# Padded operands, equal unit offsets and another block order in a hybrid decoder trunk on one core

## The chip, the core and the metric

The kernel runs on one core of one Trainium2 chip. The metric is the device time of one execution in microseconds (us), lower is better. Before the change it is 2168.96 us, the median of 3 runs (2168.53 to 2169.34). The engines are named as in the profile: PE (TensorE), PEld (its weight loads), DVE (VectorE), ACT (ScalarE), POOL (GpSimd), SP (SyncE, which issues the weight DMAs).

## The reference

Four layers act on 256 prompt rows and 8 sample rows of width 1024. Each layer has a feed-forward part, a mixer and a second feed-forward part, each followed by a layer norm. The mixers are: latent attention (layers 0 and 3), a chunked token-mixing MLP (layer 1), and multi-scale pooling (layer 2).

```python
x <- LN(alpha*x + 0.5*SwiGLU_1(x));  x <- LN(alpha*x + Mixer(x));  x <- LN(alpha*x + 0.5*SwiGLU_2(x))

# latent attention, prompt, per query block (8 heads; nope part of width 128, rotary part of width 64)
s = jnp.einsum('bqhc,bkc->bhqk', qlb, c_kv) + jnp.einsum('bqhr,bkr->bhqk', qrb, k_rope)
s = jnp.where(kpos[None, :] <= qpos[:, None], s.astype(jnp.float32) * ATTN_SCALE, NEG_INF)
# latent attention, samples: 1024 cached keys each (256 latent and 64 rotary values), gathered by pages
s_past = jnp.einsum('bqhc,bkc->bhqk', q_lat, past_ckv) + jnp.einsum('bqhr,bkr->bhqk', q_rope, past_kr)

# chunked MLP: u, v of width 3072; v normalised; 8 heads of 384
mixed = jnp.einsum('hij,bnjhd->bnihd', w_s * tril, vc) + b_s.T[None, None, :, :, None]
out = (u * mixed.reshape(B, Sp, D_CMLP)) @ w_out
```

## The kernel before

Activations lie transposed: features on the 128 partitions, and along the free axis 256 prompt columns and 8 sample columns (T = 264, SEQ = 256, DB = 8). Weights stream from memory through four stage tiles (DMA issued by SP, L171). Each is split into units: ACT casts the high part (L201), DVE subtracts to get the low part (L204). The function `mm3` multiplies each weight tile in three matmuls (L276 to L278): high weights by high activations, high by low, low by high. There are 15,144 such matmuls. A unit holds a high and a low half of 128 x 1024 and feeds 24 matmuls in the feed-forward parts. Units go round through six tiles (`NB = 6`); `room` takes tile `slot % NB` and starts `PADS[n]` floats into it (L127).

The program is written out by hand: each engine works through its instructions in the order in which they are issued, and waits by semaphores. Tile pools decide which buffer an operand gets, and so whom a write waits for. Generators interleave the prompt heads and the sample attention: each `yield` hands PE's place to another piece of work. These parts are touched:

- `start` (L391 to L420) loads the input rows and turns them by PE transposes: first the prompt's rows 0 to 127 for all 8 feature blocks k, then for each k the rows 128 to 255 (L407) and the 8 sample rows (L409). `xn` holds the prompt rows, `xs` the sample rows, `bank` and `bank_b` are PSUM tiles. ACT and DVE then make the high and low part per k (L413, L414).
- `cmlp` (layer 1): `gate(t)` (L924 to L940) multiplies for each of 24 blocks t the two prompt chunks of normalised v by the head's matrix (L928), and the 8 sample rows `vs` by the diagonal `diag` (L929).
- `mla` (layers 0 and 3): `rope` writes the rotated key `kr` (L1476) with the 64 rotary features twice, on partitions 0 to 63 and 64 to 127. `scores(h)` (L1533) adds for two query blocks the product of the nope part (L1542), the causal mask (L1543) and the rotary part (L1544), the last on 64 partitions: the lower half for even heads, the upper for odd ones.
- The sample attention handles two groups g of four samples. `flip(g, q)` transposes 32 feature rows of the cached keys of two samples on DVE (L1694 for g = 0, L1697 for g = 1) into a tile `tt`; `nat` and `natr` hold the gathered latent and rotary keys. `score(g)` (L1718) takes 20 such blocks q and issues two matmuls for each (L1740), one per sample, each on 32 weight columns, into its own 32 partitions of `sc`. `where(q)` says which samples and which feature block a q has: q 0 to 9 are all feature blocks of samples 0 and 1, q 10 to 19 those of samples 2 and 3. Up to six flips run ahead of the matmuls. L1787, the product of the probabilities with the keys, uses four column groups in turn.

Of the kernel before, what the change touches and what calls it, by code (L numbers as in the profile page):

```python
# [7 lines left out]
F32 = mybir.dt.float32  # L8
# [111 lines left out]
class Weights:  # L120
# [3 lines left out]
    NB = 6  # L124


    PADS = (0, 12, 16, 28, 36, 52)  # L127

    def __init__(self, nc, stage_pool, unit_pools):
        self.nc = nc  # L130
# [119 lines left out]
def trunk_kernel(ctx: ExitStack, tc: tile.TileContext, i: dict, o: dict, layers=None):  # L250
# [143 lines left out]
    def start():  # L394
        nc.sync.dma_start(out=ident, in_=cst("ident"))
        with tc.tile_pool(name="ld", bufs=1) as ld:
            xn = ld.tile([128, 2, D], F32, name="xn")
            xs = ld.tile([DB, D], F32, name="xs")
            for b in range(2):
                nc.sync.dma_start(out=xn[:, b, :], in_=i["x_prompt"][0, b * 128:(b + 1) * 128, :])  # L400
            nc.scalar.dma_start(out=xs, in_=i["x_sample"].rearrange("b s d -> (b s) d"))
            W.fetch()
            warm(AF.Silu)
            ps = [bank() if k < 6 else bank_b() for k in range(KD)]
            for b in range(2):
                for k, p in enumerate(ps):
                    nc.tensor.transpose(p[:, b * 128:(b + 1) * 128], xn[:, b, k * 128:(k + 1) * 128], ident)  # L407
                    if b == 1:
                        nc.tensor.transpose(p[:, SEQ:T], xs[:, k * 128:(k + 1) * 128], ident[0:DB, 0:DB])  # L409
            for k, p in enumerate(ps):  # L410
                if k == 2:
                    W.pump(1)
                S.copy(out=xh[:, k, 0:T], in_=p[:, 0:T])  # L413
                V.tensor_tensor(out=xl[:, k, 0:T], in0=p[:, 0:T], in1=xh[:, k, 0:T].bitcast(F32), op=ALU.subtract)  # L414

                nc.gpsimd.tensor_tensor(out=x[:, k, :], in0=xh[:, k, 0:T].bitcast(F32), in1=xl[:, k, 0:T].bitcast(F32), op=ALU.add)
            W.pump()
# [344 lines left out]
    def cmlp(l, j, pool, gp, prev):  # L762
        G0, B0, VB0 = 96, 0, 48
        vn = pool.tile([128, 2, DC], F32, name="vn")
        vs = pool.tile([DB, DC], F32, name="vs")
        wst = pool.tile([128, HEADS, 128], F32, name="wst")
        rb = pool.tile([128, HEADS, 136], F32, name="rb")
        bsb = pool.tile([128, HEADS, 136], F32, name="bsb")
        diag = pool.tile([DB, HEADS, DB], F32, name="diag")
        w00 = pool.tile([128, HEADS], F32, name="w00")  # L770
        stat = pool.tile([128, 3, 6, 6], F32, name="stat")
        mv = pool.tile([128, 3, 2], F32, name="mv")
# [1 line left out]
        rows = (128, 128, DB)  # L774

        def v_view(q, c):
            return vs[:, c] if q == 2 else vn[:, q, c]

        with tc.tile_pool(name="vt", bufs=3) as vt, tc.tile_pool(name="vt1", bufs=1) as vt1:
            wn = vt1.tile([128, HEADS, 128], F32, name="wn")  # L780
# [4 lines left out]
            nc.gpsimd.dma_start(out=bsb[:, :, 0:128], in_=i["b_b_s"][j:j + 1].to_broadcast([128, HEADS, 128]))  # L785
            V.memset(mv, 1.0)

            def setup(step):

                if step == 0:  # L790
                    nc.gpsimd.tensor_tensor(out=wn, in0=wn, in1=tril.unsqueeze(1).to_broadcast([128, HEADS, 128]), op=ALU.mult)
                    return
                if step == 3:
                    V.tensor_copy(out=rb[:, :, 128:136], in_=w00.unsqueeze(2).to_broadcast([128, HEADS, DB]))
                    V.tensor_copy(out=bsb[:, :, 128:136], in_=bsb[:, :, 0:1].to_broadcast([128, HEADS, DB]))
                    V.tensor_tensor(out=diag, in0=w00[0:DB].unsqueeze(2).to_broadcast([DB, HEADS, DB]),
                                    in1=ident[0:DB, 0:DB].unsqueeze(1).to_broadcast([DB, HEADS, DB]), op=ALU.mult)
                for hq in range(2):
                    f = slice(hq * 4, hq * 4 + 4)
                    p = bank()  # L800
                    if step == 1:
                        for h in range(4):
                            nc.tensor.transpose(p[:, h * 128:(h + 1) * 128], wn[:, hq * 4 + h, :], ident)
                        S.copy(out=wst[:, f, :].rearrange("p h i -> p (h i)"), in_=p)
                    if step == 2:
                        MM(p, ones, wst[:, f, :].rearrange("p h i -> p (h i)"), start=True, stop=True)
                        S.mul(out=rb[:, f, 0:128], in_=p.rearrange("p (h i) -> p h i", h=4), mul=float(D))
# [31 lines left out]
            for t in range(4, NC_T + 3):  # L839
                if t < NC_T:  # L840
                    new = [(t, bank())]
                    prev.columns(new[0][1], W.take(1)[0])
                else:
                    new = []
                    u_cols(t - NC_T)
                out = turned
                turned = [v_turn(*a) for a in acts]
                acts = v_fix(made[0:2])
                made = made[2:] + new
                for q, p in out:  # L850
                    S.copy(out=vn[:, :, q * 128:(q + 1) * 128], in_=p[:, 0:256].rearrange("p (b d) -> p b d", b=2))
                    V.tensor_copy(out=vs[:, q * 128:(q + 1) * 128], in_=p[0:DB, 256:384])
                if t == NC_T + 2:
                    break
                W.pump(min(t, W.NB))
                W.done(1)
                k, part = divmod(t - 5, 2)
                if part == 1 and 0 <= k < KD:
                    prev.affine(k)
                if part == 0 and 0 < k <= KD:  # L860
                    S.copy(out=xh[:, k - 1, 0:T], in_=x[:, k - 1, :])
                for _, g, vb in acts:
                    S.activation(out=g, in_=g, func=AF.Gelu_apprx_tanh, bias=vb)
                acts = [a[0:2] for a in acts]
                if part == 0 and 0 <= k < KD:
                    prev.normal(k)
                if part == 0 and 0 < k <= KD:
                    nc.gpsimd.tensor_tensor(out=xl[:, k - 1, 0:T], in0=x[:, k - 1, :], in1=xh[:, k - 1, 0:T].bitcast(F32),
                                            op=ALU.subtract)
                for q, _ in out:  # L870
                    if q % 4 == 3:
                        sums.extend((q // 4, r) for r in range(3))
                for a in sums[0:1]:
                    v_stats(*a)
                del sums[0:1]
                if t in (16, 17, 18, 19):
                    setup(t - 16)
# [19 lines left out]
        with tc.tile_pool(name="mx2", bufs=2) as mx2:  # L897
# [4 lines left out]
            def v_rows(q, step):  # L902
# [5 lines left out]
                        nc.sync.dma_start(out=t, in_=i[nm][j:j + 1, c].to_broadcast([DB, 512]))  # L908
                    return
                g, b = gb.pop(q)  # L910
                nc.gpsimd.tensor_tensor(out=g, in0=g, in1=vs[:, c], op=ALU.mult)
                nc.gpsimd.tensor_tensor(out=g, in0=g, in1=b, op=ALU.add)
                nc.sync.dma_start(out=o["cv"][j].rearrange("b s d -> (b s) d")[:, c], in_=g)

# [319 lines left out]
    def mla(l, j, pool, prev, stack):  # L1234
# [9 lines left out]
                mc[nm] = t[:, a - a0:a - a0 + w]  # L1244

        ckv = pool.tile([128, 2, T], F32, name="ckv")
        kr = pool.tile([128, T], F32, name="kr")
        qn = pool.tile([128, HEADS, SEQ], F32, name="qn")
        qr = pool.tile([128, 4, T], F32, name="qr")
        qs = pool.tile([128, HEADS + 3, DB], F32, name="qs")  # L1250
# [33 lines left out]
        with tc.tile_pool(name="pa", bufs=1) as pa, tc.tile_pool(name="pf0", bufs=1) as pf0, \  # L1284
# [2 lines left out]
            load_keys(0)  # L1287
            consts(("rep", "causal", "sel", "own", "new", "blk", "last"), pool)
            nc.gpsimd.memset(mx[:, 0:32], 0.0)
            nc.gpsimd.memset(qs[:, HEADS:, :], 0.0)  # L1290
            nc.gpsimd.memset(olt[:, :, HEADS:, :], 0.0)
            wukt = []
# [169 lines left out]
            def rope(key, src, r, tag, dep):  # L1462
# [8 lines left out]
                @step("o" + key, "m" + key)  # L1471
                def _():
                    t = lnp.tile([128, T], F32, tag=tag, name="rp")
                    V.tensor_tensor(out=t, in0=src(), in1=mc["ct"], op=ALU.mult)
                    V.tensor_tensor(out=sw[key], in0=sw[key], in1=mc["st"], op=ALU.mult)
                    V.tensor_tensor(out=r, in0=t, in1=sw[key], op=ALU.add)  # L1476

            for c in range(4):
                rope(str(c), lambda c=c: qp[c, 2][:, 0:T], qr[:, c, :], ("acc", "accq")[c % 2], f"p{c}2")
            rope("k", lambda: tiles[5], kr, "acc", "v5")  # L1480


            for pair in range(4):
# [33 lines left out]
        with tc.tile_pool(name="pb", bufs=1) as pb, tc.tile_pool(name="pb2", bufs=2) as pb2:  # L1517
# [15 lines left out]
            def scores(h):  # L1533
                kn = st.pop(("k", h))
                p = bank()
                off = 64 * (h % 2)
                rr = slice(off, off + 64)
                for b in range(2):
                    n = 128 * (b + 1)
                    out = p[:, 128 * b:128 * b + n]  # L1540
                    qq = slice(b * 128, (b + 1) * 128)
                    MM(out, qn[:, h, qq], kn[:, 0:n], start=True, stop=False)  # L1542
                    MM(p[:, 256 * b:256 * b + 128], identr, causal, start=False, stop=False)  # L1543
                    MM(out, qr[rr, h // 2, qq], kr[rr, 0:n], start=False, stop=True)  # L1544
                P = pb2.tile([128, 384], F32, tag="P", name="P")
                top = pb2.tile([128, 2], F32, tag="top", name="top")
                sm = pb2.tile([128, 2], F32, tag="sm", name="sm")
# [130 lines left out]
            AHEAD, ROOM = 3, 7  # L1678

            def where(q):  # L1680
                return q // 10 * 2, (q + 8) % 10

            def flip(g, q):

# [31 lines left out]
            def score(g):  # L1716
# [17 lines left out]
                for q in range(20):  # L1734
# [3 lines left out]
                        next(gens["f"])  # L1738
                    for b in range(2):
                        MM(sc[(b0 + b) * 32:(b0 + b + 1) * 32, 0:257], qbd[:, cb, b0 + b, :], tt[:, b, 0:257],  # L1740
                           start=q % 10 == 0, stop=q % 10 == 9)
                    if q % 2:
                        yield
                V.tensor_tensor(out=sc[:, 256:257], in0=sc[:, 256:257], in1=mc["new"], op=ALU.add)
# [210 lines left out]
```

## Time and profile before

| | |
|---|---|
| timed runs, median of 3 | 2168.96 us |
| profiled execution | 2157.06 us |
| its span, first to last instruction | 2155.3 us |
| mean granted clock of PE | 0.989 |
| PE busy, share of the span | 2100.6 us, 97% |
| PEld busy | 2030.7 us, 94% |
| DVE busy | 1591.1 us, 74% |
| ACT busy | 1099.2 us, 51% |
| POOL busy | 278.7 us, 13% |

Matmuls are pipelined: the duration of one record (0.28 us for a weight matmul) is longer than the interval at which the next starts (0.12 us). So intervals are read from starts, or from the pieces of the chain of waits, which lie end to end. A matmul on plain f32 operands appears as two records per instruction; a transpose or a weight matmul appears as one. In the chain, a name with a line and a count is a run of records of that line. In a timeline, the bracket at a row's end gives the engine's idle time before it and what ended that.

### The profile page before, as it was taken

The numbers are of one execution on the slowest core, as the hardware profiler recorded it, in microseconds if no ns is written. First come the engines' busy times: TensorE is split into PE (matmuls) and PEld (weight loads), VectorE is DVE, ScalarE is ACT, GpSimd is POOL, SyncE is SP. The second block draws the span as 40 slices with busy tenths as digits, with TensorE's granted clock in tenths as the row PEclk, the third lists the DMA queues.
The fourth block names the chain that finished last, engine by engine and source line by source line (L and its number), as shares of the span: only waits on it lengthen the run. The fifth ranks groups of instructions, "written<-read, shape, count | busy, mean of one in ns | idle before, by whom it ended". The sixth has DMA issues, their size and how long they took to land.

```text
span 2155.3 us, 41932 instructions
## 1 busy us (share of the span) xinstructions
PE 2100.6 (97%) x17021; PEld 2030.7 (94%) x17021; DVE 1591.1 (74%) x3135; ACT 1099.2 (51%) x1792; POOL 278.7 (13%) x321
## 2 busy tenths in 40 slices
PE   9999899999999999999999999899999999899997
PEld 8999669999999999999999999899999998579997
DVE  5546757886887797668777876998868877758774
ACT  5445636445545565455455444464555455546453
POOL 3002500000000054720000000520000005300001
PEclk9999999999999999999999999999999999999998
DMA  8556505555556544445555645356556556235551
GB/s 258 180 185 215 189 24 186 181 182 181 168 166 206 186 157 143 163 152 160 173 201 161 194 164 201 116 185 194 171 173 189 181 170 243 99 120 181 166 193 44
DMA packets 288850, 366.34 MB, mean 170 GB/s; under 512 B 7729, under 2 KB 226570, under 8 KB 286601
## 3 DMA queue, kind: packets, MB, share of 16 engines
q1 hardware_dynamic: 283200, 337.65, 48.4%
q0 software_dynamic: 5424, 25.95, 3.3%
q8 instruction: 134, 2.20, 0.4%
q14 instruction: 60, 0.48, 0.1%
q10 hardware_dynamic: 32, 0.07, 0.0%
HBM read 361.69 MB, written 2.41 MB: 169 GB/s over the span
## 4 chain that ended last, share of the span: by engine, by line
PE 93%; DVE 3%; ACT 2%; issue 1%; DMA 0%; POOL 0%; DVEq 0%; SPq 0%; ACTq 0%; POOLq 0%
PE bank L276 28%; PE bank L278 28%; PE bank L277 28%; PE bank_b L1740 2%; PE bank L1544 1%; DVE w L204 1%; PE bank L1542 1%; PE bank_b L1787 1%; PE bank L1565 1%; ACT sw L1469 1%; DVE win L1113 1%; PE bank_b L928 1%; PE bank L1528 0%; PE bank L1584 0%; ACT w L201 0%
## 5 line engine op out<-in xcount | busy, mean ns | idle before, releaser
L204 DVE TENSOR_TENSOR w<-stage,w 128x1024 fp32r<-128x1024 f32 x630 | 769.2, 1228 | 228.1 <-ACT w L201 227.0
L201 ACT CAST w<-stage 128x1024 fp32r<-128x1024 f32 x642 | 653.7, 1029 | 271.0 <-PE bank L278 216.4
L276 PE MATMUL bank<-xh,w 128*128 128x266 f32 (+1 forms) x2496 | 718.8, 288 | 2.5 <-ACT w L201 2.5
L278 PE MATMUL bank<-xh,w 128*128 128x266 f32 (+1 forms) x2496 | 716.6, 287 | 1.5 <-DVE w L204 1.5
L277 PE MATMUL bank<-xl,w 128*128 128x266 f32 (+1 forms) x2496 | 715.2, 287 | 0.0
L276 PEld LDWEIGHTS bank<-xh,w 128*128 128x128 f32 x2496 | 475.8, 191 | 3.7 <-ACT w L201 3.0
L278 PEld LDWEIGHTS bank<-xh,w 128*128 128x128 f32 x2496 | 475.0, 190 | 1.9 <-DVE w L204 1.9
L277 PEld LDWEIGHTS bank<-xl,w 128*128 128x128 f32 x2496 | 474.3, 190 | 0.3
L276 PE MATMUL bank<-hh,w 128*128 128x264 f32 x1344 | 381.4, 284 | 0.0
L278 PE MATMUL bank<-hh,w 128*128 128x264 f32 x1344 | 381.1, 284 | 0.0
L277 PE MATMUL bank<-hl,w 128*128 128x264 f32 x1344 | 381.1, 284 | 0.0
L722 ACT ACTIVATE t<-t,gb 128x264 f32<-128x264 f32 x147 | 76.1, 518 | 356.8 <-DVE t L569 356.0
L276 PEld LDWEIGHTS bank<-hh,w 128*128 128x128 f32 x1344 | 253.0, 188 | 0.0
L278 PEld LDWEIGHTS bank<-hh,w 128*128 128x128 f32 x1344 | 253.0, 188 | 0.0
L277 PEld LDWEIGHTS bank<-hl,w 128*128 128x128 f32 x1344 | 252.9, 188 | 0.0
L277 PE MATMUL bank<-zl,w 128*128 128x266 f32 (+1 forms) x736 | 212.0, 288 | 2.4 <-DVE zl L1152 2.4
L276 PE MATMUL bank<-zh,w 128*128 128x266 f32 (+1 forms) x736 | 211.8, 288 | 2.3 <-ACT zh L1148 2.3
L278 PE MATMUL bank<-zh,w 128*128 128x266 f32 (+1 forms) x736 | 211.9, 288 | 1.5 <-DVE w L204 1.5
L564 DVE COPY gb<-bank 128x2 f32<-128x2 f32 x318 | 47.0, 153 | 143.6 <-PE bank L278 143.5
L276 PEld LDWEIGHTS bank<-zh,w 128*128 128x128 f32 x736 | 140.8, 191 | 2.7 <-ACT zh L1148 2.6
L277 PEld LDWEIGHTS bank<-zl,w 128*128 128x128 f32 x736 | 140.4, 191 | 2.7 <-DVE zl L1152 2.6
L278 PEld LDWEIGHTS bank<-zh,w 128*128 128x128 f32 x736 | 140.5, 191 | 1.7 <-DVE w L204 1.7
(388 smaller groups left out, 2781.1 us busy)
## 6 DMA issues: line engine op xcount, KB each, us to landing
stage<-in_ffn_w_down_dram SPq DMA_DIRECT2D x80, 1024.0 KB
stage<-in_ffn_w_gate_dram SPq DMA_DIRECT2D x79, 1024.0 KB
stage<-in_ffn_w_up_dram SPq DMA_DIRECT2D x79, 1024.0 KB
stage<-in_b_w_in_dram SPq DMA_DIRECT2D x24, 1024.0 KB
stage<-in_b_w_out_dram SPq DMA_DIRECT2D x12, 1024.0 KB
stage<-in_a_w_o_dram SPq DMA_DIRECT2D x8, 1024.0 KB
stage<-in_ffn_w_gate_dram SPq DMA_DIRECT2D x10, 512.0 KB
stage<-in_ffn_w_up_dram SPq DMA_DIRECT2D x10, 512.0 KB
```

The costliest lines, as they stand in the source:

```text
L201: nc.scalar.copy(out=h, in_=src)
L204: engine.tensor_tensor(out=l, in0=src, in1=h.bitcast(F32), op=ALU.subtract)
L276: MM(out, wh, xh, start=start, stop=False)
L277: MM(out, wh, xl, start=False, stop=False)
L278: MM(out, wl, xh, start=False, stop=stop)
L564: V.tensor_copy(out=gb, in_=p[:, T:T + 2])
L722: S.activation(out=sg, in_=sg, func=AF.Silu, bias=vg)
L928: MM(pm[:, b * 128:(b + 1) * 128], vn[:, b, d], wst[:, h, :], start=True, stop=True)
L1113: e.tensor_tensor(out=win[q][:, :, H0:E], in0=cur[:, :, H0:E], in1=cur[:, :, H0 - d:E - d], op=ALU.add)
L1469: S.copy(out=w[b * 32:(b + 1) * 32, :], in_=src()[f * 32:(f + 1) * 32, :])
L1542: MM(out, qn[:, h, qq], kn[:, 0:n], start=True, stop=False)
L1740: MM(sc[(b0 + b) * 32:(b0 + b + 1) * 32, 0:257], qbd[:, cb, b0 + b, :], tt[:, b, 0:257], start=q % 10 == 0, stop=q % 10 == 9)
```

## The change

The change has five parts. `PADS` becomes zero for all six unit tiles. In `start` the transposes are grouped: all k of rows 0 to 127, then all k of the sample rows, then all k of rows 128 to 255. In `cmlp`, `vs` and `diag` have 128 partitions, are set to zero by POOL first, and keep their data on partitions 0 to 7; the matmul of L929 then runs over 128 partitions. In `mla` the rotary key is written once to `kr` on partitions 0 to 63 (the rest zero) and once to `kr1` on partitions 64 to 127 (the rest zero), and the rotary matmul runs over all 128 partitions with the key tile of the head's parity. Last, `where` gives q 0 and 1 the same feature block of samples 0, 1 and of samples 2, 3, then q 2 and 3 the next block, and so on; the accumulation flags follow.

```diff
-    PADS = (0, 12, 16, 28, 36, 52)
+    PADS = (0, 0, 0, 0, 0, 0)
...
-            for b in range(2):
-                for k, p in enumerate(ps):
-                    nc.tensor.transpose(p[:, b * 128:(b + 1) * 128], xn[:, b, k * 128:(k + 1) * 128], ident)
-                    if b == 1:
-                        nc.tensor.transpose(p[:, SEQ:T], xs[:, k * 128:(k + 1) * 128], ident[0:DB, 0:DB])
+            for k, p in enumerate(ps):
+                nc.tensor.transpose(p[:, 0:128], xn[:, 0, k * 128:(k + 1) * 128], ident)
+            for k, p in enumerate(ps):
+                nc.tensor.transpose(p[:, SEQ:T], xs[:, k * 128:(k + 1) * 128], ident[0:DB, 0:DB])
+            for k, p in enumerate(ps):
+                nc.tensor.transpose(p[:, 128:256], xn[:, 1, k * 128:(k + 1) * 128], ident)
...
-        vs = pool.tile([DB, DC], F32, name="vs")
+        vs = pool.tile([128, DC], F32, name="vs")
-        diag = pool.tile([DB, HEADS, DB], F32, name="diag")
+        diag = pool.tile([128, HEADS, DB], F32, name="diag")
...
+            nc.gpsimd.memset(vs, 0.0)
+            nc.gpsimd.memset(diag, 0.0)
...
         kr = pool.tile([128, T], F32, name="kr")
+        kr1 = pool.tile([128, SEQ], F32, name="kr1")
...
+            nc.gpsimd.memset(kr[64:128, :], 0.0)
+            nc.gpsimd.memset(kr1[0:64, :], 0.0)
...
-                    V.tensor_tensor(out=r, in0=t, in1=sw[key], op=ALU.add)
+                    if key == "k":
+                        V.tensor_tensor(out=kr[0:64, :], in0=t[0:64, :], in1=sw[key][0:64, :], op=ALU.add)
+                        V.tensor_tensor(out=kr1[64:128, :], in0=t[64:128, 0:SEQ], in1=sw[key][64:128, 0:SEQ], op=ALU.add)
+                    else:
+                        V.tensor_tensor(out=r, in0=t, in1=sw[key], op=ALU.add)
...
-                off = 64 * (h % 2)
-                rr = slice(off, off + 64)
+                rk = (kr, kr1)[h % 2]
...
-                    MM(out, qr[rr, h // 2, qq], kr[rr, 0:n], start=False, stop=True)
+                    MM(out, qr[:, h // 2, qq], rk[:, 0:n], start=False, stop=True)
...
-                return q // 10 * 2, (q + 8) % 10
+                return q % 2 * 2, (q // 2 + 8) % 10
...
-                           start=q % 10 == 0, stop=q % 10 == 9)
+                           start=q < 2, stop=q > 17)
```

At the start of the program PE's order before is this (`xn` the prompt rows, `xs` the sample rows; rows that repeat the pair are left out):

```order
L407 MATMUL bank<-ident,xn 128x128 x6
L407 MATMUL bank_b<-ident,xn 128x128 x2
L407 MATMUL bank<-ident,xn 128x128
L409 MATMUL bank<-ident,xs 128x8
...
L407 MATMUL bank_b<-ident,xn 128x128
L409 MATMUL bank_b<-ident,xs 128x8
L276 MATMUL bank<-xh,w 128x264
```

And now, with the lines of the changed file:

```order
L406 MATMUL bank<-ident,xn 128x128 x6
L406 MATMUL bank_b<-ident,xn 128x128 x2
L408 MATMUL bank<-ident,xs 128x8 x6
L408 MATMUL bank_b<-ident,xs 128x8 x2
L410 MATMUL bank<-ident,xn 128x128 x6
L410 MATMUL bank_b<-ident,xn 128x128 x2
L276 MATMUL bank<-xh,w 128x264
```

The sample transposes have moved ahead of the second half of the prompt's, in one group.

In layer 0's mixer, DVE's order from the rotated key to the first copies into `qbd` before is this (`w` and `tt` are the tiles that flips write, `top` and `sm` belong to the prompt's softmax):

```order
L1476 TENSOR_TENSOR kr<-rp,sw 128x264
L1694 STREAM_TRANSPOSE w<-natr 128x2x256 x2
L1548 TENSOR_REDUCE top<-bank 128x1
L1549 TENSOR_REDUCE top<-bank 128x1
L1550 TENSOR_TENSOR top<-top,rq 128x2
L1647 COPY qlat<-bank_b 128x2x64
L1609 RECIPROCAL sm<-sm 128x2
L1694 STREAM_TRANSPOSE w<-nat 128x2x256
L1694 STREAM_TRANSPOSE tt<-nat 128x2x256 x3
L1724 COPY qbd<-qrep 32x40x8 x2
```

And now (`kr_2253` is the tile `kr1`):

```order
L1485 TENSOR_TENSOR kr<-rp,sw 64x264
L1486 TENSOR_TENSOR kr_2253<-rp,sw 64x256
L1705 STREAM_TRANSPOSE w<-natr 128x2x256 x2
L1559 TENSOR_REDUCE top<-bank 128x1
L1560 TENSOR_REDUCE top<-bank 128x1
L1561 TENSOR_TENSOR top<-top,rq 128x2
L1658 COPY qlat<-bank_b 128x2x64
L1620 RECIPROCAL sm<-sm 128x2
L1705 STREAM_TRANSPOSE w<-natr 128x2x256
L1705 STREAM_TRANSPOSE tt<-natr 128x2x256
L1705 STREAM_TRANSPOSE tt<-nat 128x2x256 x2
L1735 COPY qbd<-qrep 32x40x8 x2
```

One DVE instruction is added, the number of flips and their places among the other instructions stay, and the four rotary blocks (`natr`) are now flipped first for all four samples.

## Rows read from the trace of the kernel before

**Rows 1.** The page: busy totals, and the chain that ended last by engine.

```profile
PE 2100.6 (97%) x17021; PEld 2030.7 (94%) x17021; DVE 1591.1 (74%) x3135; ACT 1099.2 (51%) x1792; POOL 278.7 (13%) x321
...
PE 93%; DVE 3%; ACT 2%; issue 1%; DMA 0%; POOL 0%; DVEq 0%; SPq 0%; ACTq 0%; POOLq 0%
```

**Rows 2.** Timeline of PE at one gate: start us, us, instruction, idle before.

```profile
827.45 0.61 PE L928 MATMUL bank_b<-wst,vn 128*128 128x128 f32 x4
827.99 0.38 PE L929 MATMUL bank_b<-diag,vs 8*128 8x8 f32 x2
828.30 0.39 PE L276 MATMUL bank<-xh,w 128*128 128x264 f32 x1
828.53 0.28 PE L277 MATMUL bank<-xl,w 128*128 128x264 f32 x1
```

**Rows 3.** Timeline of PE: two short passes of full rows, then another.

```profile
231.88 0.37 PE L1397 MATMUL bank_b<-rsq,ones 128*128 128x8 f32 x2
232.10 0.69 PE L1421 MATMUL bank_b<-rsq,ones 128*128 128x264 f32 x2
```

**Rows 4.** Chain of waits in layer 0's mixer: start us, us, what.

```profile
269.58 3.61 PE bank_b L1740 x32
...
308.94 1.73 PE bank L1565 x8
...
316.72 3.59 PE bank_b L1787 x64
```

**Rows 5.** Timeline of PE over one head's prompt scores.

```profile
300.12 0.49 PE L1542 MATMUL bank<-kn,qn 128*128 128x128 f32 x2
300.36 0.30 PE L1543 MATMUL bank<-causal,identr 128*128 128x128 f32 x1
300.60 0.48 PE L1544 MATMUL bank<-kr,qr 64*128 64x128 f32 x2
301.01 0.70 PE L1542 MATMUL bank<-kn,qn 128*128 128x256 f32 x2
...
302.33 1.13 PE L1528 MATMUL bank<-ckv,stage 128*128 128x256 f32 x4
```

**Rows 6.** Timeline of ACT: the copy into qbd.

```profile
256.81 1.55 ACT L1722 COPY qbd<-qrep 32x320 f32<-32x320 f32 x2
```

**Rows 7.** Windows of PE: us, busy (instructions), clock, DMA share, GB/s; three units, then six.

```profile
568.52:571.47 2.95, 2.95 (x26) 1.00 1.03 338
571.47:574.46 2.99, 2.99 (x26) 1.00 0.88 297
580.40:583.33 2.93, 2.93 (x26) 1.00 1.07 346
568.52:586.30 17.78, 17.78 (x147) 1.00 0.71 224
```

**Rows 8.** Timeline of DVE: flips of the first and of the second half.

```profile
270.35 1.30 DVE L1694 STREAM_TRANSPOSE tt<-nat 128x512 f32<-128x512 f32 x2
...
280.55 2.03 DVE L1697 STREAM_TRANSPOSE tt<-w 128x256 f32<-128x256 f32 x6
```

**Rows 9.** Timeline at the start.

```profile
10.52 1.23 DVE L204 TENSOR_TENSOR w<-stage,w 128x1024 fp32r<-128x1024 f32 x1 [1.40 <-ACT w L201]
...
11.81 0.59 PE L276 MATMUL bank<-xh,w 128*128 128x264 f32 x1
...
12.42 0.42 PE L278 MATMUL bank<-xh,w 128*128 128x264 f32 x1
```

**Rows 10.** POOL by shapes, 243 to 336 us: zeros of qbd.

```profile
L1515 POOL MEMSET qbd<- 128x1280 f32 x1 | 1.2, 1163 | 0.0
```

**Rows 11.** Windows: us, busy of PE, PEld, DVE, ACT, POOL, clock, DMA share, GB/s.

```profile
273.50:276.95 3.45, 1.26 (x8) 0.92 (x9) 2.00 (x10) 0.99 (x4) 0.00 (x0) 1.00 0.01 2
276.95:280.40 3.45, 2.83 (x13) 1.54 (x13) 3.40 (x12) 1.88 (x3) 0.19 (x1) 0.51 0.01 3
727.00:760.00 33.00, 33.00 (x268) 32.73 (x268) 31.18 (x71) 22.19 (x41) 8.30 (x9) 1.00 0.59 176
```

More of the change, by code (lines that the diff above doesn't have):

```diff
@@ L776, in v_view @@
         def v_view(q, c):
-            return vs[:, c] if q == 2 else vn[:, q, c]
+            return vs[0:DB, c] if q == 2 else vn[:, q, c]
         with tc.tile_pool(name="vt", bufs=3) as vt, tc.tile_pool(name="vt1", bufs=1) as vt1:
@@ L795, in setup @@
                     V.tensor_copy(out=bsb[:, :, 128:136], in_=bsb[:, :, 0:1].to_broadcast([128, HEADS, DB]))
-                    V.tensor_tensor(out=diag, in0=w00[0:DB].unsqueeze(2).to_broadcast([DB, HEADS, DB]),
+                    V.tensor_tensor(out=diag[0:DB], in0=w00[0:DB].unsqueeze(2).to_broadcast([DB, HEADS, DB]),
                                     in1=ident[0:DB, 0:DB].unsqueeze(1).to_broadcast([DB, HEADS, DB]), op=ALU.mult)
@@ L851, in cmlp @@
                     S.copy(out=vn[:, :, q * 128:(q + 1) * 128], in_=p[:, 0:256].rearrange("p (b d) -> p b d", b=2))
-                    V.tensor_copy(out=vs[:, q * 128:(q + 1) * 128], in_=p[0:DB, 256:384])
+                    V.tensor_copy(out=vs[0:DB, q * 128:(q + 1) * 128], in_=p[0:DB, 256:384])
                 if t == NC_T + 2:
@@ L910, in v_rows @@
                 g, b = gb.pop(q)
-                nc.gpsimd.tensor_tensor(out=g, in0=g, in1=vs[:, c], op=ALU.mult)
+                nc.gpsimd.tensor_tensor(out=g, in0=g, in1=vs[0:DB, c], op=ALU.mult)
                 nc.gpsimd.tensor_tensor(out=g, in0=g, in1=b, op=ALU.add)
@@ L1475, in _ @@
                     V.tensor_tensor(out=sw[key], in0=sw[key], in1=mc["st"], op=ALU.mult)
-                    V.tensor_tensor(out=r, in0=t, in1=sw[key], op=ALU.add)
+                    if key == "k":
[3 more added lines that the diff above has]
+                        V.tensor_tensor(out=r, in0=t, in1=sw[key], op=ALU.add)
             for c in range(4):
                 rope(str(c), lambda c=c: qp[c, 2][:, 0:T], qr[:, c, :], ("acc", "accq")[c % 2], f"p{c}2")
-            rope("k", lambda: tiles[5], kr, "acc", "v5")
+            rope("k", lambda: tiles[5], None, "acc", "v5")
             for pair in range(4):
```

## Prediction

> **What bounds the kernel now.** I read the totals first, then the chain of waits by engine, then the timeline at each edited line, then windows over whole weight units. The totals show TensorE (PE) busy for 97% of the span, and the chain that ended last is PE for 93% [rows 1]. So time is saved only where PE itself issues sooner, and VectorE (DVE) matters where it is late for PE. DMA carries 0% of the chain. The sum below is made against the profiled execution, 2157.06 us (span 2155.3), and carried over as a difference to the median of the runs, 2168.96.
>
> **1. Gate rows padded (L929).** The 8-row matmul stands between 128-row ones. From the first pass of L928 to the second matmul after L929 lie 828.53 − 827.45 = 1.08 us [rows 2], for four passes of L928, two of L929 (each fp32 instruction here is two records) and one weight matmul. What would it be without gaps? A pass of 128 rows and 8 columns takes half of 232.10 − 231.88 = 0.22, that is 0.11 us [rows 3]; a pass of 256 columns 1.73 / 8 = 0.216, so one of 128 columns 0.108 [rows 4]; the weight matmul 17.78 / 144 = 0.12 [rows 7]. That is 4 × 0.108 + 2 × 0.11 + 0.12 = 0.77, and 1.08 − 0.77 = 0.31 goes, with loads hidden. L929 has 48 records, 24 instructions, all in layer 1: 24 × 0.30 = **7.2 us**. Ends: 0 (loads stay exposed) to 8. What is late next there is PE's own next matmul.
>
> **2. Rope keys padded (L1544).** One head's prompt scores take 302.33 − 300.12 = 2.21 us [rows 5]. Contiguous, five passes of 128 columns (two L1542, one L1543, two L1544) and four of 256 plus one L1543 are 5 × 0.108 + 4 × 0.216 + 0.108 = 1.51. So 0.70 us a head, a little more if L1543, one record, is shorter than I count. There are 8 heads in each of two layers, 16 × 0.70 = 11.2. Head 1 gains nothing: the sample scores behind it start when ScalarE has filled qbd at 258.36 [rows 6], and PE starts them at 258.45 already. That takes 2 × 0.70 off; a few heads end on sample matmuls of 32 columns, where a change of shape stays, about −0.3. With the upside of L1543, **10.0 us**; ends 0 and 12.8 (0.80 × 16).
>
> A rule of the Trainium skill speaks against both terms: "TensorE: Matmul & The Clock Gate", section "Part 3: Packing small matmuls", says that a weight load overlaps running matmuls only when its row group differs; a 128-row load would then never hide, and both terms would be zero. The trace disagrees: in the L1565 run each full 128-row pass takes 0.216 us with its load inside, while the 64-row pass starts 300.60 − 300.36 = 0.24 us after L1543, a single pass of 128 columns [rows 4, 5].
>
> **3. Sample scores (L1740).** The edit of `where` lets two successive key blocks q use all four column groups in turn instead of two. Now 16 instructions take 3.61 us, 0.226 each; L1787, which goes through four groups in turn, takes 3.59 for 32, 0.112 each [rows 4]. There are 320 records, 160 instructions: 160 × 0.114 = 18.2 us at most. Not all is reached, for the operands are made by DVE. A flip costs 1.30 / 2 = 0.65 us a block in the first half and 2.03 / 3 = 0.68 in the second [rows 8], three times what PE will need for one (0.226). Walking through one layer with these durations and DVE's order: in the first half PE waits for q9 and q11 (0.4) and for q18 and q19, whose flips stand behind the row maxima of head 2 (1.1); in the second half q0 to q3 are already paced by flips (0.7 of the 0.9 lost), and q11 to q13 now are (0.9). That leaves 9.1 − 3.1 = 6.0 a layer, **12.0 us**; ends 0 (flips pace everything) and 18.2. The order of samples changes which keys are wanted when, but before the second half's flips the DMA share is 0.01 already [rows 11].
>
> **4. Pads to 0.** The six unit tiles now start at equal offsets. The trace shows that the interval of matmuls depends on the slot and repeats from round to round: six units of 24 matmuls take 17.78 us, the quickest slot 2.93 and the slowest 2.99 [rows 7], or 122.1 to 124.6 ns a matmul. The slots differ only in address. With one offset, all six become alike; the distance from the moving tile xh to the weights becomes that of the first slot, 2.95. Then 17.78 − 6 × 2.95 = 0.08, which is 0.5 ns a matmul; with the finer times of these starts 0.7 ns, over the 5,520 matmuls on xh and xl: 2.9 to 3.9 us. I take **3.5**. The matmuls on hh and zh, zl I leave at nothing. Ends: every unit on xh like the quickest, −1.35 ns, 7.5 us gained; like the slowest, +1.2 ns, 6.5 us lost.
>
> The page "SBUF — State Buffer", section "SBUF: two separate sides", says that of the engines only VectorE and GpSimd hold each other up and PE waits on no one. By that rule the pads are worth nothing and the sum is 3.5 us smaller; the unit windows show 0.06 us between slots that it leaves unexplained.
>
> **5. First transposes.** Now the last pair ends as the first weight matmul starts, 11.81. The low weights are finished by DVE at 10.52 + 1.23 = 11.75; the matmul on these, the third, starts at 12.42 [rows 9]. With the 8-row loads grouped I expect the transposes to end before that, and DVE's 11.75 is late next: the third matmul gains up to 0.67, and later casts keep some of it. I take **0.3**, ends 0 and 0.67.
>
> **Costs.** The keys' sum becomes two DVE instructions of half the rows, ahead of the first flips, with the queries' matmuls between those and the first sample score: nothing; without that cover not more than a flip's 0.65 us a layer. The zeros of kr and kr1 stand on GpSimd before work nobody waits for. The zeros of vs: 1.16 us for 1280 elements [rows 10] makes 2.8 for 3072, in front of the layer's mean subtraction; PE is busy 33.00 of 33.00 us there [rows 11]. In all I take **−0.3**, ends 0 and −2.
>
> Sum: 7.2 + 10.0 + 12.0 + 3.5 + 0.3 − 0.3 = 32.7 us. Profiled execution 2157.1 − 32.7 = 2124.4; median 2169.0 − 32.7 = 2136.3.
>
> The clock adds a blur. After one PE-poor stretch (1.26 busy of 3.45 us) the granted clock was 0.51, its lower level of 1.2 GHz, for 3.45 us with PE 2.83 busy [rows 11]. At the upper level half of that would do. So a stretch costs up to 1.4 us; shorter waits may remove one, more idle between blocks may add one: ±3.
>
> **Rivals.**
> (a) Padded rows buy nothing, because loads stay exposed. Terms 1 and 2 go: 2136.3 + 17.2 = 2153.5. For it: the rule above. Against: full-row passes back to back, long and short ones [rows 3, 4]. Chance 0.06.
> (b) The flips pace PE through all sample scores: term 3 falls to about 3, 2145. For it: 0.65 against 0.226. Against: DVE has idle time between blocks, and other PE work stands between them. Chance 0.09.
> (c) Addresses decide nothing (the rule of term 4 as a mechanism): 2140. Against: the repeating slot times. Chance 0.13.
> (d) Slower. Equal offsets bring the moving tile and the weights of every family to a bad distance. The price is 15,144 weight matmuls × 1 ns = 15.1 us per ns. From 2139.8 without term 4, it passes 2173.3 (slower by 0.2%) at 2.2 ns more on all of them; at 2.5 ns it is 2178. For it: an address effect of 2.5 ns is seen between slots. Against: the slowest slot seen lies 1.2 ns over the mean, and no family would have to leave what was seen. Chance 0.04.
> My forecast, with clock and small terms: 0.68, own range 2127 to 2145.
>
> **Numbers.** Predicted 2136. To the own range (a) and (b) add the upper end: 2124 to 2151. A change under 0.2% (4.3 us) can't be told from none here; slower: (d), 0.04; within 0.2%: all three large terms failing at once, 0.04; faster 0.92.
>
> **What would show it.** In the new profile: no gap around the gate's third matmul (0.77 for the stretch that took 1.08); the head's scores about 1.5 us; a run of 16 sample instructions near 1.8 us where flips are ready; unit windows on xh all near 2.95; the third weight matmul before 12. The forecast is wrong if 128-row loads stay visible around L929 and L1544, if DVE ends nearly every wait in the sample scores, or if unit windows come out above 3.0.

## The result, and the profile after

The changed kernel took 2132.81 us (median of 4 runs, 2131.80 to 2133.66) beside 2169.15 us for the kernel before (2168.53 to 2171.03): ratio 0.9831, 95% interval 0.9814 to 0.9848, or 36.3 us less. Forecast were 2136 and 32.7 us less. Timed once more, the changed kernel stayed at 2132.19, but the kernel before came to 2155 to 2163 in four later sets, and the same comparison gave 0.9861 (0.9841 to 0.9882), 30 us by the ratio. The two first profiles differ by only 2157.06 − 2133.66 = 23.4 us; for the profiled execution the forecast was 2124.4. Much of what follows is about why the kernel before differs from one set of runs to the next.

The totals of the page, and the chain by engine, which answer to [rows 1]:

```profile
PE 2072.2 (97%) x17021; PEld 2014.4 (94%) x17021; DVE 1593.9 (75%) x3137; ACT 1098.6 (52%) x1792; POOL 281.2 (13%) x327
...
PE 92%; DVE 4%; ACT 2%; issue 1%; DMA 0%; SPq 0%; POOL 0%; DVEq 0%; ACTq 0%; POOLq 0%
```

PE is busy 28.4 us less than before and still 97% of the span; DVE's share of the chain went from 3% to 4%.

The gate in PE's timeline [rows 2]:

```profile
820.01 0.61 PE L932 MATMUL bank_b<-wst,vn 128*128 128x128 f32 x4
820.46 0.29 PE L933 MATMUL bank_b<-diag,vs 128*128 128x8 f32 x2
820.60 0.37 PE L276 MATMUL bank<-xh,w 128*128 128x264 f32 x1
820.80 0.28 PE L277 MATMUL bank<-xl,w 128*128 128x264 f32 x1
```

From the first pass of L932 to the second matmul behind the gate it is 820.80 − 820.01 = 0.79 us, where it was 1.08. The forecast had 0.77. The weight loads (PEld) of the short matmul and of the one behind it, before and then now:

```profile
827.99 0.29 PEld L929 LDWEIGHTS bank_b<-diag,vs 8*128 8x128 f32 x2
828.30 0.19 PEld L276 LDWEIGHTS bank<-xh,w 128*128 128x128 f32 x1
...
820.35 0.30 PEld L933 LDWEIGHTS bank_b<-diag,vs 128*128 128x128 f32 x2
820.57 0.19 PEld L276 LDWEIGHTS bank<-xh,w 128*128 128x128 f32 x1
```

Before, each of these loads begins together with its matmul (827.99 and 828.30). Now it begins ahead of it, by 0.11 and 0.03 us, while the passes in front still run.

One head's prompt scores in PE's timeline [rows 5]:

```profile
297.43 0.49 PE L1553 MATMUL bank<-kn,qn 128*128 128x128 f32 x2
297.68 0.31 PE L1554 MATMUL bank<-causal,identr 128*128 128x128 f32 x1
297.82 0.44 PE L1555 MATMUL bank<-kr,qr 128*128 128x128 f32 x2
298.09 0.60 PE L1553 MATMUL bank<-kn,qn 128*128 128x256 f32 x2
298.34 0.41 PE L1554 MATMUL bank<-causal,identr 128*128 128x128 f32 x1
298.59 0.65 PE L1555 MATMUL bank<-kr,qr 128*128 128x256 f32 x2
299.07 0.38 PE L1540 MATMUL bank<-ckv,stage 128*128 128x256 f32 x1
```

It takes 299.07 − 297.43 = 1.64 us; before 2.21, forecast 1.51. The rotary pass now starts 0.14 us after the mask's, not 0.24.

Runs of sample scores in the chain of waits of layer 0 (start us, us, what), to compare with the first piece of [rows 4]:

```profile
260.33 2.41 PE bank_b L1751 x24
...
277.55 2.82 PE bank_b L1751 x13
...
289.92 1.51 PE bank_b L1751 x23
...
296.06 1.44 PE bank_b L1751 x24
```

The last run has 12 instructions in 1.44 us, 0.120 each, about half of the 0.226 before; the third has 0.131. The first two are slower. The first ran at the lower clock (2.41 us for 12), which will come up. The second lies in another stretch at that clock (0.50 from 275.9 to 282.7 us), in which DVE with its flips was busy 3.35 of the first 3.40 us; so the clock slows it, and probably the flips too.

Unit windows of PE on xh, the same units as in [rows 7], then six together:

```profile
561.66:564.60 2.94, 2.94 (x27) 1.00 1.03 342
564.60:567.54 2.94, 2.94 (x27) 1.00 0.90 301
573.42:576.36 2.94, 2.94 (x27) 1.00 1.05 349
561.66:579.30 17.64, 17.64 (x147) 1.00 0.71 228
```

All are 2.94 now, and six take 17.64 instead of 17.78.

The start, as in [rows 9]:

```profile
10.44 1.22 DVE L204 TENSOR_TENSOR w<-stage,w 128x1024 fp32r<-128x1024 f32 x1 [1.14 <-ACT w L201]
...
10.46 0.59 PE L276 MATMUL bank<-xh,w 128*128 128x264 f32 x1 [0.89 <-ACT w L201]
...
11.72 0.59 PE L278 MATMUL bank<-xh,w 128*128 128x264 f32 x1 [0.45 <-DVE w L204]
```

The first weight matmul starts 1.35 us earlier, the third 0.70.

One place stands out as a wait. The first row maximum of head 0 (L1559) on DVE, in the timeline of all engines:

```profile
248.59 0.65 PE L1555 MATMUL bank<-kr,qr 128*128 128x256 f32 x2
...
249.64 0.95 POOL L1281 DMA_INDIRECT w<-in_cache_kv_latent_dram,idx  x1 [0.30 <-issue]
250.59 0.77 POOL L535 TENSOR_TENSOR x<-mean,x 128x264 f32<-128x264 f32 x1
251.44 0.74 POOL L536 TENSOR_TENSOR x<-x,negr 128x264 f32<-128x264 f32 x1
252.02 0.29 DVE L1559 TENSOR_REDUCE top<-bank 128x1 f32<-128x128 f32 x1 [3.76 <-PE bank L1540]
...
253.14 1.08 PE L1669 MATMUL bank_b<-qlat,c_rep 128*128 128x72 f32 x8 [2.60 <-issue]
```

PE ends the head's scores at 249.24 and DVE has nothing else to do, yet its instruction starts at 252.02, near the end of GpSimd's second tensor instruction (252.18 as recorded; times on GpSimd are rough). In the first profile of the kernel before, the same wait was 1.14 us. PE, which needs a copy that DVE makes right after (L1658), idles 2.60 us before L1669. And this is what the clock did next (windows: us, busy of PE, PEld, DVE, ACT, POOL, granted clock, DMA share, GB/s):

```profile
252.05:255.46 3.41, 2.32 (x21) 2.35 (x22) 2.33 (x8) 1.81 (x6) 1.24 (x2) 1.00 1.02 418
255.46:258.87 3.41, 3.41 (x17) 3.32 (x16) 2.07 (x4) 1.59 (x3) 1.17 (x6) 0.50 0.22 89
258.87:262.29 3.42, 3.42 (x24) 1.63 (x27) 1.89 (x5) 2.71 (x9) 0.21 (x2) 0.50 0.00 0
```

After PE's idle time from 250.54 to 253.14 and a stretch with 2.32 of 3.41 us busy, the clock is at its lower level of 1.2 GHz for 6.8 us, over head 1's scores and the first sample run.

### The profile page after: what moved, and what is told of

Its sections match the earlier page's. It is cut to its first block, busy times and chain, and to the rows that moved or that the text cites. A ratio compares the mean times of both kernels' runs of the same rounds, so it can differ in the third digit from the quotient of the medians.

```text
span 2131.9 us, 41916 instructions
## 1 busy us (share of the span) xinstructions
PE 2072.2 (97%) x17021; PEld 2014.4 (94%) x17021; DVE 1593.9 (75%) x3137; ACT 1098.6 (52%) x1792; POOL 281.2 (13%) x327
## 3 DMA queue, kind: packets, MB, share of 16 engines
HBM read 361.69 MB, written 2.41 MB: 171 GB/s over the span
## 4 chain that ended last, share of the span: by engine, by line
PE 92%; DVE 4%; ACT 2%; issue 1%; DMA 0%; SPq 0%; POOL 0%; DVEq 0%; ACTq 0%; POOLq 0%
PE bank L278 28%; PE bank L276 28%; PE bank L277 28%; PE bank_b L1751 1%; DVE w L204 1%; PE bank_b L1798 1%; PE bank L1576 1%; ACT sw L1477 1%; PE bank L1553 1%; PE bank L1555 1%; DVE win L1117 1%; PE bank_b L932 1%; ACT w L201 0%; PE bank L1540 0%; PE bank L1595 0%
## 5 line engine op out<-in xcount | busy, mean ns | idle before, releaser
L204 DVE TENSOR_TENSOR w<-stage,w 128x1024 fp32r<-128x1024 f32 x630 | 771.1, 1232 | 224.6 <-ACT w L201 224.2
L567 DVE SCALAR_TENSOR_TENSOR t<-mean,gb,bank 128x264 f32<-128x264 f32 x318 | 141.1, 483 | 0.7
L276 PEld LDWEIGHTS bank<-zh,w 128*128 128x128 f32 x736 | 140.0, 190 | 1.6 <-ACT zh L1152 1.5
```

The source lines that it names most:

```text
L204: engine.tensor_tensor(out=l, in0=src, in1=h.bitcast(F32), op=ALU.subtract)
L276: MM(out, wh, xh, start=start, stop=False)
L567: V.scalar_tensor_tensor(out=t, in0=self.mean, scalar=gb[:, 0:1], in1=p[:, 0:T], op0=ALU.mult, op1=ALU.subtract)
```

## The experiments

All runs were timed in rounds against the kernel before on the same chip. There were four sets, each on another chip: e1 to e4, e5 to e8, e9 to e11, and e12. The medians of the kernel before in them were 2155.31, 2160.63, 2160.36 and 2163.47 us.

| run | edit | median, us | ratio to before, 95% interval | wait of the first row maximum, layers 0 and 3, us |
|---|---|---|---|---|
| first profiles | none / all of the change | | | 1.14, 1.12 / 2.78, 2.76 |
| e1 | none | 2155.74 | 1.0005 (0.9996 to 1.0014) | 0.04, 0.04 |
| e2 | pads | 2151.38 | 0.9986 (0.9975 to 0.9996) | 0.04, 0.04 |
| e3 | gate | 2147.04 | 0.9968 (0.9957 to 0.9980) | 0.04, 0.04 |
| e4 | block order | 2144.21 | 0.9950 (0.9937 to 0.9963) | 0.04, 0.04 |
| e5 | all of the change | 2132.19 | 0.9861 (0.9841 to 0.9882) | 1.21, 1.26 |
| e6 | pads and rope keys | 2148.72 | 0.9939 (0.9920 to 0.9957) | 1.22, 1.19 |
| e7 | all but block order | 2140.77 | 0.9902 (0.9884 to 0.9921) | 1.27, 1.29 |
| e8 | first transposes | 2162.42 | 0.9995 (0.9980 to 1.0010) | 1.19, 1.82 |
| e9 | all, gathers split | 2125.86 | 0.9839 (0.9825 to 0.9853) | 0.04, 0.04 |
| e10 | gathers split | 2154.15 | 0.9969 (0.9957 to 0.9980) | 0.04, 0.04 |
| e11 | all but rope keys | 2136.00 | 0.9892 (0.9875 to 0.9908) | 1.25, 1.19 |
| e12 | all but rope keys, gathers split | 2132.65 | 0.9861 (0.9845 to 0.9878) | 0.04, 0.04 |

The last column is the start of the first row maximum less the end of its last matmul, from the traces: one execution of each run.

**e1, the kernel before once more.**

> The kernel before once more, unchanged, with a second profile, because its first profiled execution (2157.06 us) lay 12 us under its timed runs (2168.5 to 2171.0), while the changed kernel's profiled execution (2133.66) lies among its timed runs. Theory A (the first profile is one rare quick execution): the new profiled execution is near 2169 and the 12 us more than in the first trace lie in a few places, mean granted clock under 0.989. Theory B (a profiled execution of this kernel is always quicker than a timed one): the new profile is near 2157 again with clock 0.989. Ratio 1.000 in both.

Its profiled execution was 2154.97 us, its median 2155.74, so profiled and timed runs agree here: neither theory held as put. The 2169 was not the rule; the kernel before ranged from 2152 to 2171 over all sets. Aligned matmul by matmul, the traces of unchanged code agree to 0.1 us outside the two latent-attention layers and the first 50 us. All else that differs lies in those two layers. One place is the row maximum. Here it started at once (timeline of all engines in e1):

```profile
248.01 0.95 POOL L1275 DMA_INDIRECT w<-in_cache_k_rope_dram,idx  x1 [0.30 <-issue]
...
248.22 0.70 PE L1544 MATMUL bank<-kr,qr 64*128 64x256 f32 x2
...
248.95 0.29 DVE L1548 TENSOR_REDUCE top<-bank 128x1 f32<-128x128 f32 x1 [1.62 <-PE bank L1544]
...
249.27 0.94 POOL L1275 DMA_INDIRECT w<-in_cache_kv_latent_dram,idx  x1 [0.30 <-issue]
...
249.60 0.78 DVE L1550 TENSOR_TENSOR top<-top,rq 128x2 f32<-128x2 f32 x1
```

The head's matmuls end at 248.92, and the row maximum starts at 248.95, just as a gather of GpSimd ends (248.96) and before the next begins. The next two-input instruction of DVE (L1550) then takes 0.78 us (0.16 in e10, where no gather runs beside it) and ends 0.17 us after the following gather. In the first profile of before the row maximum was 1.14 us late.

**e2 to e4, single parts.** The edits are the lines of the diff that belong to each (`PADS`; `vs` and `diag`; `where` and its flags).

> The kernel before with the pads of the six unit tiles at zero, nothing else. Theory A (the interval follows the distance of moving tile and weights): 2.9 to 3.9 us faster, 0.9982 to 0.9987, and every unit window on xh near 2.95 us. Rival (addresses decide nothing, the slots' times come from something else): 1.0000 and windows from 2.93 to 2.99 as before.

> The kernel before with vs and diag on 128 partitions alone. Theory A: 24 gates at 0.30 us, 7.2 us faster, ratio 0.9967. Rival (loads of 128 rows stay exposed): 1.0000. If the timed difference of the whole change (36 us) holds 12 us that no single part brings, this part alone shows 7 us and not more.

> The kernel before with the new order of sample score blocks alone. Theory A: 12 us faster, ratio 0.9945. Rival (flips on DVE pace the scores; the two traces on hand show the two latent-attention layers together 12.4 us shorter, with the rope keys' part in it): about 5 us, 0.998. A third way, that this part also changes how often the clock drops: more than 14 us, below 0.9935, and fewer low-clock stretches between 250 and 300 us than in the kernel before.

Pads: 3.0 us by the ratio (0.9 to 5.4), as theory A had it; in this trace too the units on xh take 2.94 us each, so the offset of its tile set a slot apart. Whether it acts by the distance from the moving tile, as the theory has it, or by itself, these runs do not separate. Counted in the aligned traces outside the latent-attention layers it is 4.6. Gate: 6.9 us; the aligned traces put 6.8 us between the gates' first and last matmul. Block order: 10.8 us (8.0 to 13.6), close to theory A (12), and not the 5 of the rival; flips pace some blocks, not all.

**e5 to e8, combinations.** e5 is the changed kernel; e6 and e7 are the diff's parts as named; e8 is the hunk in `start`.

> The changed kernel once more, timed in rounds with the kernel before on one chip. So far its ratio is 0.983 (36 us) with the kernel before at 2169; the second set of runs has the kernel before at 2155, and single parts at -6.9 (gate), -10.8 (score order) and -3.0 (pads). Theory A (parts add up: 6.9 + 10.8 + 3.0 + about 10 for the rope keys + 0.3): 31 us, ratio 0.9856. Rival (the two first traces tell the whole): 23.4 us, 0.989. Third way (the 36 us are real wherever it runs): 0.983.

> The kernel before with pads at zero and the padded rope keys; against e2_pads0 it shows the keys alone. Theory A: 10.0 us from the keys, so 13 under the kernel before, 0.9940. Rival (128-row loads hide, but the heads' scores then wait for the softmax on DVE and ACT): 5 us from the keys, 0.9963.

> The changed kernel with the old order of sample score blocks. Theory A: against the changed kernel it is slower by what the order brings alone (10.8), so 20 us under the kernel before, 0.9905. Rival (the flips pace the scores once the keys' matmuls are short, so order and keys share one gain): it is only 5 us slower than the changed kernel, 0.988.

> The kernel before with the first transposes regrouped, nothing else. Theory A: the first weight matmul starts about 1.3 us earlier, the third 0.6, and 0.3 us is left at the end; ratio 0.9999, below what can be told. Rival (the first trace of the changed kernel is 0.9 to 1.4 us ahead from the start on, and all of it stays): 1.0 us, 0.9995. What tells them apart is the trace: how far ahead its matmuls are at 12, 50 and 160 us.

e5: 30.0 us by the ratio (28.4 by the medians), where theory A had 31. e6: 0.9939, as theory A had it (0.9940); less the 3.0 us of the pads, that is 10 us for the keys by the ratios. In absolute times e6 is only 2.7 us under e2, and the table says why the two must not be compared so: in the set of e1 to e4 the row maximum was on time in all four kernels, in the set of e5 to e8 it was late in all four, and the kernel before was 5 us slower there. So in these traces, one a run, the wait goes by the set and not by the edit, and only ratios within a set compare like with like. e7: the order is worth 8.6 us within this set, 10.8 alone. e8: nothing that can be told (0.9980 to 1.0010). Its first weight matmul is 1.3 us ahead of the first profile's, but the third only 0.05 (12.36 against 12.42), not the 0.6 expected: L204 took 1.82 us there instead of 1.23, beside a two-input instruction of GpSimd (L417, 9.78 to 11.23). At the 300th weight matmul 0.3 is left, less than the 0.55 that two runs of unchanged code differ by there.

**e9 and e10, the gathers moved.** The fence shows the edit, in the changed kernel and in the one before.

```diff
-                load_keys(1)
+                load_keys(1, ((0, 1), (1, 1), (2, 1), (3, 1), (0, 0), (1, 0)))
...
                     for a in ahead:
                         own_key(*a)
+                    load_keys(1, ((2, 0), (3, 0)))
```

`load_keys` now takes pairs of sample and kind (1 the rotary keys, 0 the latent ones).

> The changed kernel, but the gathers of the second sample group are issued by GpSimd in two parts: the four of rotary keys and the latent ones of two samples where they stood, the latent ones of the other two samples behind the first own-key copies. In all ten traces so far DVE's first row maximum of head 0 starts when a GpSimd instruction ends: 0.04 us behind its matmul in five, 1.1 to 2.8 us late in the other five, and the changed kernel is always among the late ones; PE then idles and the clock drops near 255 us. Theory A (GpSimd's descriptors or its reads hold DVE off): with two gathers fewer ahead of it the wait is 0 to 0.6 us in both layers, 1 to 2.5 us a layer gained, with the clock drop at 255 gone 2 to 5; in all 4 to 10 us under the changed kernel, 2122 to 2128. Rival (DVE waits for its own instructions or for PE's signal, and GpSimd's ends only fall together with it): the wait stays 1.2 to 2.8 us and the time 2132.

> The kernel before with the same split of the gathers. Its times have ranged from 2152 to 2171 us. Theory A (whether DVE's first row maximum slips past a gather or is held by it is decided by some 20 ns, and the held case brings low-clock stretches): with the gathers out of the way it is never held, its times are narrow and near the quick end, 2148 to 2154. Rival: as wide as before, median 2155 to 2161.

(Of the ten traces then on hand, four had the row maximum at once and six late, as the table shows; the expectation's "five" was miscounted.) In both kernels and both layers the wait is gone. The changed kernel gains 6.3 us by the medians of two sets (2132.19 to 2125.86), 4.8 by the ratios (0.0022 × 2160), and is the quickest version of all. The kernel before gains 6.2 us by the medians of one set and is narrow now, 2152.77 to 2155.13 in seven runs, beside 2156.49 to 2165.09 for the unsplit one. Timeline of all engines in e9:

```profile
243.42 0.94 POOL L1281 DMA_INDIRECT w<-in_cache_kv_latent_dram,idx  x1 [0.30 <-issue]
...
245.90 1.17 POOL L1527 MEMSET qbd<- 128x1280 f32 x1
...
249.25 0.65 PE L1555 MATMUL bank<-kr,qr 128*128 128x256 f32 x2
...
249.94 0.29 DVE L1559 TENSOR_REDUCE top<-bank 128x1 f32<-128x128 f32 x1 [1.01 <-PE bank L1555]
...
251.06 1.98 PE L1669 MATMUL bank_b<-qlat,c_rep 128*128 128x72 f32 x16
```

GpSimd is through by 247.07, DVE starts 0.04 us after the matmuls' modelled end, and PE goes on without a gap. The edit does more than move two gathers: it also puts the rotary ones first. The first two gathers of the changed kernel, and then the second of e9:

```profile
236.86 1.03 POOL L1281 DMA_INDIRECT w<-in_cache_k_rope_dram,idx  x1 [0.44 <-PE bank L278]
241.84 0.95 POOL L1281 DMA_INDIRECT w<-in_cache_kv_latent_dram,idx  x1 [3.95 <-PE bank L278]
...
238.37 0.99 POOL L1281 DMA_INDIRECT w<-in_cache_k_rope_dram,idx  x1 [0.30 <-issue]
```

In the old order the second gather, a latent one, came 3.95 us late, and all of GpSimd's work behind it with it; in the new one GpSimd goes on after 0.30 us. Its second tensor instruction (L536) ends at 245.96 instead of 252.18, 6.2 us earlier, of which the two moved gathers with their pauses make 2.5. So the runs show that the wait goes when GpSimd is done before the scores are; the new order alone was not tried.

The clock over the same work as above stays up:

```profile
249.90:253.30 3.40, 3.40 (x29) 3.12 (x27) 2.28 (x8) 1.82 (x6) 0.00 (x0) 1.00 0.10 41
253.30:256.70 3.40, 2.82 (x24) 2.39 (x27) 2.84 (x8) 2.22 (x4) 1.68 (x7) 1.00 0.00 0
256.70:260.10 3.40, 3.40 (x42) 1.84 (x36) 3.24 (x8) 3.40 (x11) 2.43 (x9) 1.00 0.60 176
```

How much of the gain is the wait and how much the clock is not separated, for the one did not always come with the other. The window behind the held row maximum in the first profile of before (wait 1.14 us), and the same place in e1 (wait 0.04):

```profile
253.40:256.80 3.40, 3.40 (x31) 3.33 (x30) 2.50 (x5) 1.08 (x3) 0.60 (x2) 1.00 1.03 422
...
254.90:258.30 3.40, 3.40 (x13) 1.60 (x14) 1.81 (x6) 2.81 (x6) 1.17 (x7) 0.50 0.29 111
```

The clock stayed up behind the wait in the one, and fell without the wait in the other. Nor does the set decide alone: in the set of e9 to e11 the quickest run of the unsplit kernel before (2156.49) had a mean granted clock of 0.989 and the slowest (2165.09) 0.986. That the wait is what set the kernel before of the first set of experiments (2155) apart from the later ones (2160 to 2163) is therefore not shown; its timed runs left no traces.

**e11 and e12, the rope keys left out.** Both are the changed kernel with the hunks on `kr` undone, e12 with the split gathers too.

> The changed kernel with the rotary keys on 64 rows as before, pads zero and all else changed. Theory A of the prediction: 10 us slower than the changed kernel, 2142. Rival, after e6_pads0_kr (2.7 us from the keys alone) : the second DVE instruction for kr1 pushes the first row maximum into the gathers, the wait and the lower clock eat most of what the padded matmuls save; 1 to 4 us slower, 2133 to 2136, with the heads' scores each 0.7 to 0.8 us longer in the trace and no wait behind the gathers.

> The kernel of e9_split_after with the rotary keys on 64 rows again: what the padded keys bring where the first row maximum is not held by the gathers. By the traces a head's scores take 2.21 us on 64 rows and 1.64 on 128, so 16 heads hold 9 us, 14 of them 8. Theory A (free of the wait, the keys bring what the matmuls save): 8 to 9 us slower than e9 (2125.9), 2134. Rival (the heads' time is hidden behind flips and softmax anyway): 2 to 4 us slower, 2128 to 2130. If the keys' second DVE instruction is what lengthens the wait, e11 to e12 brings less than the 6.3 us that the split brought the changed kernel.

By the ratios the keys bring 0.0031 × 2160 = 6.7 us with the wait (e5 to e11), 4.8 without it (e9 to e12); by the medians, where the sets differ, 3.8 and 6.8. With e6's 10 the ratios give 5 to 10 us, and each figure is a difference of two ratios, uncertain by some 5 us. Theory A of e11 (10 us, 2142) lies above both, though within that uncertainty. The traces are finer. Between e12 and e9 seven of the eight heads of a layer get 0.48 to 0.57 us shorter and head 1 not at all, 7.6 us over both layers. Against that stands a later start of the first head, here in the first profile of before and in e7:

```profile
247.71 0.49 PE L1542 MATMUL bank<-kn,qn 128*128 128x128 f32 x2 [0.17 <-issue]
...
248.95 0.49 PE L1553 MATMUL bank<-kn,qn 128*128 128x128 f32 x2 [0.60 <-DVE kr L1486]
```

In both, PE starts about 0.52 us after the key's last write on DVE, and with the second instruction that write comes later: 0.43 us more idle time, in each of the two layers. That leaves 7.6 − 0.9 = 6.7 us. The rival of e11, that the second DVE instruction for `kr1` brings the wait about, falls: e11 has no such instruction and waits 1.25 us.

## Why the prediction was right, and where it was not

The direction, the time and, but for the keys, the sizes of the parts were right. That the median came within 4 us of the forecast is in part luck. The sum was made against the profiled execution, and there it missed: 2133.66 instead of 2124.4, or 23.4 us gained instead of 32.7. It was then carried over to a median 12 us higher, as if the profiled execution were quicker than the timed ones in both kernels; in the changed kernel it was not. The better test of the sum is e5 with the single parts. Point by point:

- **What bounds it.** PE's own work: right. 28 us less of it, and the time fell with it.
- **Gate, 7.2 us.** 24 × (1.08 − 0.79) = 7.0 by the rows, 6.9 by e3. The rival of exposed loads (a) is refuted: gates and heads both got shorter, and at the gate the 128-row loads begin ahead of their matmuls.
- **Rope keys, 10.0 us.** The mechanism was right, the size somewhat high. By the rows a head gains 2.21 − 1.64 = 0.57, not 0.70: from start to start, the four passes of 128 columns in L1553 and L1555 take 0.52 us where I counted 0.43, and the mask's matmul 0.14 where I counted 0.108. All heads make 7.6, with nothing for head 1, as I had said. The second DVE instruction, which I put at nothing, cost 0.43 us a layer, because the first head's scores wait for it. That leaves 6.7; the ratios give 5 to 10.
- **Block order, 12.0 us.** 10.8 alone, 8.6 within the change. The chain's run of 12 shows the mechanism (0.120 each), and the gain stays well under the 18.2 us of all blocks at that pace, as forecast: flips hold some of them (at 270.08 us one stands in the chain for 0.72 us, ahead of the scores). Rival (b), flips pacing everything, is refuted.
- **Pads, 3.5 us.** 3.0 by e2, 4.6 by the aligned traces outside latent attention. All units became alike, as forecast, and rivals (c) and (d) are refuted. That the distance to the moving tile is what counts was not tested apart from the offset itself.
- **First transposes, 0.3 us.** In the changed kernel 0.70 at the third matmul, as the bound had it; in e8, with this edit alone, 0.05. Not to be told at the end in either.
- **The clock, ±3 us.** In the changed kernel's profile the wait before 253 us was followed by 6.8 us at the lower level; in e9, without the wait, there is none at that place. The wait itself was in my trace, as PE's idle time of 1.5 us before L1658, and I did not ask what held DVE. In the first profiles it was longer in the changed kernel, 2.78 and 2.76 us beside 1.14 and 1.12, and the clock fell behind it there alone. That can account for much of the 9.3 us by which the profiled execution missed, and it goes beyond the ±3 that I allowed; the share is not isolated.

The parts alone sum to 3.0 + 6.9 + 10.8 us and 5 to 10 for the keys, so 26 to 31, and the whole gave 30.0 in e5: forecast 32.7. The 36.3 of the first measurement is more than the parts bring. The kernel before stood at 2169 there, above its medians in all four later sets, while the changed kernel stood where it always did; its first profile, too, was 12 us quicker than the timed runs it was set beside. What the kernel before did in that set can't be told, since no profile of a run at 2169 exists. That the row maximum was held longer there, with more time at the lower clock, would fit e8 and e10, and is not shown.

## What to carry to other kernels

An operand with few rows between full ones costs its neighbours' weight loads: padding with zeros gave back 0.3 us a time at the gate and 0.5 to 0.6 a head for most heads. The price is a memset, and for the keys a second write that the first head waits for. A wait whose releaser had long been done is worth an experiment of its own: reordering GpSimd's gathers and moving two of them brought 5 to 6 us, nearly as much as the 24 padded gates. And where an unchanged kernel differs from set to set by as much as the effect sought, only ratios within a set are compared.

## What was not expected of the hardware

DVE's row maximum reads PSUM and writes one column, and no instruction of its queue stood before it. Still it was held in 7 of the 14 traces, in both layers each time, while GpSimd was busy. It then started 0.05 to 0.25 us before the recorded end of a GpSimd instruction, and in the three kernels in which GpSimd was done before the scores it was never held. In e1 to e4, where it was on time, a gather ended within 0.03 us of its start. GpSimd's instructions alone do not explain it: in the changed kernel's first profile GpSimd paused from 249.34 to 249.64, after the scores' end at 249.24, and the row maximum did not start in that pause.

The Trainium skill, "SBUF — State Buffer", section "SBUF: two separate sides", says that DVE and GpSimd share a port pair as an exclusive lock, which a DVE instruction takes in a two-port mode, or with two SBUF inputs against a GpSimd instruction that reads SBUF. L1550, which has two SBUF inputs and took 0.78 us instead of 0.16 beside a gather in e1, agrees with that if a gather reads SBUF, which no run here shows. L1476, also with two SBUF inputs, does not: it took 0.43 us inside a gather in e1 (245.68 to 246.11), and its counterpart in e12 0.43 beside a memset alone. The row maximum, with one input from PSUM, isn't a two-input instruction. Why it is held, and why copies and transposes beside other gathers were not, stays open.
